# A transformer stack's feed-forward second projections as seven block products of 2x2 blocks

## The chip, the cores and the metric

One core of a Trainium2 chip runs the whole program. The time is device microseconds (us) of one execution, the median of several runs. Engines: TensorE (PE in the profile, PEld its weight loads), VectorE (DVE), ScalarE (ACT), GpSimd (POOL), SyncE (SP, which issues the weight loads from DRAM).

## The reference

512 tokens of width 1024 pass through two blocks of one kind and one of a second kind, all in float32. Each has a token mixer (attention) and feed-forwards; what the change touches are the four feed-forwards. Cut to these, with `rms_norm` and the convolution as in the model:

```python
def conv_ffn(h, w_up, conv_w, conv_b, w_down):      # twice: f0, f1
    u = h @ w_up                                    # 512x1024 @ 1024x5632
    u = causal_conv_of_width_3(u, conv_w) + conv_b  # per channel, along tokens
    gate, up = jnp.split(u, 2, axis=-1)
    return (jax.nn.gelu(gate, approximate=True) * up) @ w_down   # 512x2816 @ 2816x1024

def _swiglu(x, w_gate, w_up, w_down):               # twice: s0, s1
    return (jax.nn.silu(x @ w_gate) * (x @ w_up)) @ w_down

x = x + rms_norm(f, g_post)      # f: a feed-forward's result; 0.5 * in s0 and s1
h = rms_norm(x, g_pre_of_next)
```

## The kernel before, in words

Stages run in the order m0, f0, m1, f1, s0, m2, s1: m are the mixers, f the feed-forwards with convolution and gelu, s those with silu. Every float32 operand of a matmul is held as a high part (rounded to the matmul's format fp32r) and a low part (the rest), and each product of two tiles is three matmuls: high x high, high x low, low x high (`mm3`, L223 to L225). The high part of a tile is a copy on ScalarE, the low part a difference on VectorE (`split2`, L231 and L232; for weights `_split`, L112, and `flush`, L121).

**Weights** come through one stream. `Weights` holds a list of chunks (1 MB in DRAM, loaded by SP into two raw buffers `wraw`) and of units (128x1024, in one of four slots `whi`, `wlo`). A unit's place in the list is the order of its use. When the last unit of a chunk has its low part, SP is told to load the chunk after the next into that buffer (`_load`, from `flush`). `ahead` splits units while slots are free.

**A feed-forward** (`ffn`) goes through its 22 inner tiles of 128 in two parts of 11 (`reg_ffn`). For each inner tile, a gate tile and an up tile (128 inner x 512 tokens) are summed over 8 k-tiles in a PSUM bank. `convd` (L622 to L624) makes the convolution with one ScalarE and two VectorE passes; then come gelu on ScalarE, and `gg = cg * cu` on GpSimd (L641). Without convolution, silu on ScalarE and `gg = cg * PS` on VectorE (L643). `split2` puts the tile into `gh` and `gl`. At the part's end `out_part` makes the second projection: for each half of the 1024 output columns, four token tiles x 11 inner tiles x 3 matmuls of 128x128 by 128x512. The first part's result is copied to `part`; the second part's is added to it (`post1`: addition L672, ScalarE's sum of squares L673, the product with the gain L674, on VectorE for the first half and on GpSimd for the second).

**The junction.** In the second half of the last part (`out_last`) the weights' low parts go to GpSimd (`W.defer`, `W.lo`), three more slots are lent for the next stage's first weights, and as each token tile is complete, `finish` (L574 to L587) makes the root of its mean square (L580, L326, L582), adds the scaled result to x in two halves (L585), and `pre_norm` makes the normed row `hn` for the next stage (L335 square sum, L339). `turn` (L380) transposes hn on TensorE, and `evacuate` splits the transposed tile into `Hh` and `Hl`. The next stage starts with tokens 0 and 1 (L422, L460) while 2 and 3 are finished.

Every engine takes its instructions in the order in which the program issues them; no scheduler reorders them.

Of the kernel before, what the change touches and what calls it, by code (L numbers as in the profile page):

```python
# [16 lines left out]
T = 512  # L17
# [10 lines left out]


class Weights:  # L30

# [5 lines left out]
    def __init__(self, nc, pool):  # L37
        self.nc = nc
        self.raw = [pool.tile([128, 2048], F32, name=f"wraw{i}") for i in range(self.NRAW)]
        self.free = self.slots(pool, self.NHL, "w")  # L40
        self.extra, self.first, self.limit = [], 0, 0
        self.where = {}
        self.chunks = []
        self.units = []
        self.loaded = 0
# [25 lines left out]
    def add(self, srcs, a, b, unit_slices):  # L71
        c = len(self.chunks)
        self.chunks.append((srcs, a, b))
        for n, (a0, a1, b0, b1) in enumerate(unit_slices):
            self.units.append((c, a0, a1, b0, b1, n == len(unit_slices) - 1))

# [26 lines left out]
    def _split(self):  # L103
        u = self.split
        c, a0, a1, b0, b1, last = self.units[u]
        _, a, b = self.chunks[c]
        if c >= self.loaded:
            self.flush()
        raw = self.raw[c % self.NRAW][:, :a * b].rearrange("p (a b) -> p a b", a=a)[:, a0:a1, b0:b1]
# [3 lines left out]
        self.late.append((lo, raw, hi, c + self.NRAW if last else 0))  # L113
        self.split += 1
        if not self.defer:
            self.flush()

    def flush(self):

        for lo, raw, hi, nxt in self.late:  # L120
            self.lo.tensor_sub(lo, raw, hi.bitcast(F32))  # L121
            self._load(nxt)
        self.late = []

    def ahead(self, keep=1):

        self.flush()
        while self.split < len(self.units):
# [8 lines left out]
    def view(self, u):  # L137
        _, a0, a1, b0, b1, _ = self.units[u]
        n = (a1 - a0) * (b1 - b0)
        return tuple(t[:, :n].rearrange("p (a b) -> p a b", a=a1 - a0) for t in self.where[u])  # L140

# [32 lines left out]
class Net:  # L174
# [418 lines left out]
    def reg_ffn(self, wg, wg0, wu, wu0, wd):  # L593
        W = self.W
        for k0, nk in ((0, 11), (11, 11)):
            for j in range(k0, k0 + nk, 2):
                m = min(2, k0 + nk - j)
                W.cols(wg, wg0 + j * 128, m * 128)
                W.cols(wu, wu0 + j * 128, m * 128)
            for h in range(2):  # L600
                W.rows(wd, k0, nk, h * 512, 512)

    def ffn(self, conv, half, last, gpost, gpre_next):
# [3 lines left out]
        with ExitStack() as st:  # L607
            P = st.enter_context(self.tc.tile_pool(name="ffn", bufs=1))
            gh = P.tile([128, 11, T], F32R, name="gh")
            gl = P.tile([128, 11, T], F32R, name="gl")  # L610
            part = P.tile([128, 4, D], F32, name="part")
            tmp = ExitStack()
            Q = tmp.enter_context(self.tc.tile_pool(name="ffntmp", bufs=1))
            cg = [Q.tile([128, T], F32, name=f"cg{i}") for i in range(3)]
            gg = [Q.tile([128, T], F32, name=f"gg{i}") for i in range(2)]
            if conv is not None:
                cu = [Q.tile([128, T], F32, name=f"cu{i}") for i in range(3)]
                cw = Q.tile([128, 2 * NFT, 4], F32, name="cw")
                nc.gpsimd.dma_start(cw, conv)

            def convd(dst, ps, j):
# [4 lines left out]
            def post_g(j):  # L626
                def f(ps):
                    c = cg[j % 3]
                    if conv is not None:
                        convd(c, ps, j)  # L630
# [5 lines left out]
            def post_u(j, jj):  # L636
                def f(ps):
                    g = gg[j % 2]
                    if conv is not None:
# [9 lines left out]
            sst = self.sm(8)  # L649
            for p in range(2):  # L650
                k0 = p * 11
                for jj in range(0, 11, 2):
                    m = min(2, 11 - jj)
                    posts = [post_g(k0 + jj + e) for e in range(m)] + [post_u(k0 + jj + e, jj + e) for e in range(m)]
                    if p == 0 and jj == 0:
# [3 lines left out]
                    for f in posts:  # L659
                        self.gemm_T(f, soon=True)  # L660
                if p == 0:
                    for h in range(2):
                        def post0(i, ps):
                            if i % 2:
                                nc.vector.tensor_copy(part[:, i, h * 512:h * 512 + 512], ps)
                            else:
                                nc.scalar.activation(part[:, i, h * 512:h * 512 + 512], ps, AF.Copy)
                        self.out_part((gh, gl), 11, post0)
                else:
                    def post1(i, ps, h):  # L670
                        f = part[:, i, h * 512:h * 512 + 512]
                        nc.vector.tensor_add(f, ps, f)  # L672
                        nc.scalar.activation(ps, f, AF.Square, accum_out=sst[:, h * 4 + i:h * 4 + i + 1])  # L673
                        (nc.gpsimd if h else nc.vector).tensor_mul(f, f, self.gpost[:, h * 512:h * 512 + 512])  # L674

                    tmp.close()
                    with self.tc.tile_pool(name="more", bufs=1) as M:
                        self.W.lend(self.W.slots(M, 3, "m"), 9)
                        self.out_last((gh, gl), 11, lambda i, ps: post1(i, ps, 0), lambda i, ps: post1(i, ps, 1),
                                      lambda i: self.finish(i, part[:, i, :512], part[:, i, 512:], sst[:, i:i + 1],  # L680
                                                            sst[:, 4 + i:5 + i], half, last))
                        self.W.give_back()
                    while self.side:
                        self.pump()

# [1068 lines left out]
```

## Time and profile before

| | |
|---|---|
| median of 3 runs | 2851.55 us (2850.07 to 2852.74) |
| the profiled execution | 2851.37 us |
| its span, first to last instruction | 2849.4 us |
| TensorE busy | 2790.2 us (98%), 14196 matmuls |
| VectorE, ScalarE, GpSimd busy | 1397.4, 1102.0, 365.3 us |
| mean granted TensorE clock | 0.995 |
| DMA | 255.45 MB, mean 90 GB/s |

The page gives each engine's busy time; the timeline lists instructions with their start, their duration and, in brackets, how long the engine was idle before and which operand came last; the waits group such idle times. TensorE's matmuls overlap, so one's duration (0.39) is longer than the distance of two starts.

### The profile page before, as it was taken

To read this page: it belongs to the slowest core of one execution; us is meant where nothing else is said; L and a number is where in the kernel's file an instruction comes from. 1 tells how busy PE (TensorE), PEld (TensorE's weight loads), DVE (VectorE), ACT (ScalarE), POOL (GpSimd) and SP (SyncE) were. 2 spreads that over 40 slices of the span, in tenths; PEclk is the share of its full clock that TensorE was granted. 3 is DMA by queue.
4 is the path that set the end of the run, shared out by engine and by line. 5 is a ranking of instruction groups with operands and counts; after the bars stand their busy time and mean duration, and the time that the engine had idled before them with its cause. 6 is when DMAs were issued, how large, how long until landed. Compare 5 with 4: busy or idle time off the path is not lost.

```text
span 2849.4 us, 34641 instructions
## 1 busy us (share of the span) xinstructions
PE 2790.2 (98%) x14196; PEld 2282.4 (80%) x14196; DVE 1397.4 (49%) x2126; ACT 1102.0 (39%) x1886; POOL 365.3 (13%) x285
## 2 busy tenths in 40 slices
PE   8999999999999999999999999999999999999998
PEld 7778688888878787788888888888777978888887
DVE  4666645535555666455535453233653343533334
ACT  3444634423444456444334332223343322432232
POOL 5221100100122221000101110000522000000000
PEclk9999999999999999999999999999999999999999
DMA  4211132333322111233332323323421223322332
GB/s 148 74 57 34 34 130 86 105 115 108 111 71 91 60 38 45 82 119 95 108 103 91 110 89 100 100 81 118 140 74 53 72 78 97 111 94 92 104 97 73
DMA packets 234318, 255.45 MB, mean 90 GB/s; under 512 B 33072, under 2 KB 193184, under 8 KB 233776
## 3 DMA queue, kind: packets, MB, share of 16 engines
q1 hardware_dynamic: 228016, 233.53, 25.7%
q0 software_dynamic: 4992, 16.94, 1.9%
q8 instruction: 111, 1.82, 0.3%
q10 hardware_dynamic: 1152, 2.77, 0.3%
q14 instruction: 47, 0.39, 0.0%
HBM read 248.60 MB, written 5.53 MB: 89 GB/s over the span
## 4 chain that ended last, share of the span: by engine, by line
PE 90%; DVE 5%; ACT 3%; issue 1%; DMA 0%; DVEq 0%; ACTq 0%; POOL 0%; POOLq 0%
PE PS L223 26%; PE PS L225 25%; PE PS L224 25%; PE PS L422 2%; DVE x L585 2%; PE PS L1124 1%; PE PS L1110 1%; PE PS L1080 1%; PE PS L425 1%; PE PS L460 1%; DVE hn L339 1%; PE PS L1220 1%; PE PS L1192 1%; PE PS L380 1%; PE PS L1511 1%
## 5 line engine op out<-in xcount | busy, mean ns | idle before, releaser
L121 DVE TENSOR_TENSOR wlo<-wraw,whi 128x1024 fp32r<-128x1024 f32 (+3 forms) x366 | 440.3, 1208 | 726.5 <-ACT whi L112 726.4
L223 PE MATMUL PS<-Hh,whi 128*128 128x512 f32 x1952 | 776.1, 398 | 4.1 <-DVE oBl L232 2.8
L225 PE MATMUL PS<-Hh,wlo 128*128 128x512 f32 x1952 | 761.0, 390 | 0.9 <-DVE wlo L121 0.9
L224 PE MATMUL PS<-Hl,whi 128*128 128x512 f32 x1952 | 760.6, 390 | 0.0
L112 ACT ACTIVATE whi<-wraw 128x1024 fp32r<-128x1024 f32 (+2 forms) x432 | 436.9, 1016 | 340.0 <-PE PS L225 279.5
L223 PEld LDWEIGHTS PS<-Hh,whi 128*128 128x128 f32 x1952 | 366.5, 188 | 88.3 <-issue 8.7
L225 PEld LDWEIGHTS PS<-Hh,wlo 128*128 128x128 f32 x1952 | 366.4, 188 | 79.2 <-DVE wlo L121 1.5
L224 PEld LDWEIGHTS PS<-Hl,whi 128*128 128x128 f32 x1952 | 367.0, 188 | 70.5
L121 POOL TENSOR_TENSOR wlo<-wraw,whi 128x1024 fp32r<-128x1024 f32 (+1 forms) x66 | 162.8, 2467 | 1268.1 <-ACT whi L112 1268.1
L223 PE MATMUL PS<-whi,gh 128*128 128x512 f32 x624 | 242.8, 389 | 0.0
L224 PE MATMUL PS<-wlo,gh 128*128 128x512 f32 x624 | 242.7, 389 | 0.0
L225 PE MATMUL PS<-whi,gl 128*128 128x512 f32 x624 | 242.7, 389 | 0.0
L231 ACT ACTIVATE gh<-gg 128x512 fp32r<-128x512 f32 x88 | 55.7, 632 | 327.2 <-DVE gg L643 178.9
L223 PEld LDWEIGHTS PS<-whi,gh 128*128 128x128 f32 x624 | 117.3, 188 | 24.3
L225 PEld LDWEIGHTS PS<-whi,gl 128*128 128x128 f32 x624 | 117.1, 188 | 24.4
L224 PEld LDWEIGHTS PS<-wlo,gh 128*128 128x128 f32 x624 | 117.1, 188 | 24.4
L641 POOL TENSOR_TENSOR gg<-cg,cu 128x512 f32<-128x512 f32 x44 | 56.7, 1289 | 549.4 <-DVE cu L624 549.4
L232 DVE TENSOR_TENSOR gl<-gg,gh 128x512 fp32r<-128x512 f32 x88 | 60.9, 693 | 125.6 <-ACT gh L231 125.6
L223 PE MATMUL PS<-whi,Hh 128*128 128x512 f32 (+2 forms) x320 | 118.2, 369 | 1.9 <-ACT whi L112 1.6
L224 PE MATMUL PS<-wlo,Hh 128*128 128x512 f32 (+2 forms) x320 | 116.7, 365 | 0.5 <-DVE wlo L121 0.5
L225 PE MATMUL PS<-whi,Hl 128*128 128x512 f32 (+2 forms) x320 | 116.5, 364 | 0.0
L1091 DVE TENSOR_REDUCE small<-PS 128x2 f32<-128x256 f32 (+3 forms) x64 | 52.7, 824 | 72.0 <-PE PS L1082 61.2
(355 smaller groups left out, 3966.0 us busy)
## 6 DMA issues: line engine op xcount, KB each, us to landing
wraw<-in_w_in_dram SPq DMA_DIRECT2D x56, 1024.0 KB, 5.0
wraw<-in_w_up_dram SPq DMA_DIRECT2D x40, 1024.0 KB, 5.1
wraw<-in_ffn_w_gate_dram SPq DMA_DIRECT2D x20, 1024.0 KB, 5.2
wraw<-in_ffn_w_up_dram SPq DMA_DIRECT2D x20, 1024.0 KB, 5.3
wraw<-in_w_down_dram SPq DMA_DIRECT2D x16, 1024.0 KB, 5.0
wraw<-in_ffn_w_down_dram SPq DMA_DIRECT2D x16, 1024.0 KB, 5.0
wraw<-in_w_out_dram SPq DMA_DIRECT2D x12, 1024.0 KB, 4.9
wraw<-in_w_down_dram SPq DMA_DIRECT2D x8, 768.0 KB, 4.3
```

Source lines behind the costliest of these rows:

```text
L112: self.nc.scalar.activation(hi, raw, AF.Copy)
L121: self.lo.tensor_sub(lo, raw, hi.bitcast(F32))
L223: mm(out, lh, rh, start=start, stop=False)
L224: mm(out, lh, rl, start=False, stop=False)
L225: mm(out, ll, rh, start=False, stop=stop)
L231: nc.scalar.activation(hi, src, AF.Copy)
L232: nc.vector.tensor_sub(lo, src, hi.bitcast(F32))
L339: nc.vector.scalar_tensor_tensor(hn, self.x[:, i], r, self.gpre, op0=OP.mult, op1=OP.mult)
L422: self.nc.tensor.matmul(ps[:, sl], ww[:, k], self.Hh[:, k, sl], start=k == 0 and ww is w[0], stop=False)
L585: nc.vector.scalar_tensor_tensor(x, f, r, x, op0=OP.mult, op1=OP.add)
L641: nc.gpsimd.tensor_mul(g, cg[j % 3], cu[j % 3])
L1091: nc.vector.reduce_max(m, S2, axis=AX.X, negate=True)
```

## The change

The second projection of one part, G (512 tokens x 2P inner tiles) times W (2P inner tiles x 1024), is taken as 2x2 blocks: tokens 0 to 255 and 256 to 511; even and odd inner tiles; columns 0 to 511 and 512 to 1023. With A11, A12 (tokens' first half, even and odd tiles), A21, A22, and B11 to B22, seven products of blocks make the four blocks of the result (Winograd's form):

S1 = A21 + A22, S2 = S1 - A11, S3 = A11 - A21, S4 = A12 - S2; T1 = B12 - B11, T2 = B22 - T1, T3 = B22 - B12, T4 = B21 - T2. In the order of the program: product 0 A11 x B11 (bank pair a), 1 S1 x T1 (b), 2 S2 x T2 (onto a), 3 S4 x B22 (onto b), 4 A12 x B21 (c), 5 S3 x T3 (onto a), 6 A22 x T4 (onto a).

A product is two token tiles x P pairs of inner tiles x 3 matmuls. For this the parts become three, of 6, 8 and 8 inner tiles (P = 3, 4, 4).

- The sums S are four GpSimd operations of 128x256 for each pair of inner tiles (L773 to L778), in the buffers `hn`, and are split with A11, A12 and A22 into `Ah` and `Al`. Splits are issued one tile later (`late`, `run_late`).
- The differences T are GpSimd operations in the raw buffers (L114, L115, L116, L118). B11 and B12 come by the stream; B22 and B21 are loaded into `tm`, the buffers of cg, cu and gg, when the part's last tile is through (`open_quad`, L130). The weight units of a part are, in order, B11, T1, T2, B22, B21, T3, T4, two to each at P = 4.
- After each product its bank is copied to or added to `part` (L701, L703, L705); the result blocks that need no further product are finished (`fin`) after products 3, 4, 5 and 6.
- In the last part low parts go to GpSimd from product 4 on; three of `Ah`/`Al`'s operands that are done are lent as slots; tokens 0 and 1 are transposed in product 6.

```diff
-        for k0, nk in ((0, 11), (11, 11)):
+        for k0, nk in self.PARTS:
...
-            for h in range(2):
-                W.rows(wd, k0, nk, h * 512, 512)
+            W.quad(wd, k0, nk // 2)
...
+        order(b11, [lambda i: sub(b11(i), b12(i), b11(i))])
+        order(b11, [lambda i: when_open(lambda: sub(b11(i), b22(i), b11(i)))()])
+        order(b11, [lambda i: sub(b12(i), b22(i), b12(i))])
+        order(b22, [])
+        order(b21, [lambda i: sub(b21(i), b21(i), b11(i)), lambda i: self._load(c + 2) if i == last else None])
+        order(b12, [lambda i: self._load(c + 3) if i == last else None])
+        order(b21, [])
...
+        steps = ((0, a, False, 0, 0, True, False), (3, b, False, 1, 1, True, False), (4, a, True, 0, 1, True, False),
+                 (6, b, True, 0, 1, False, True), (1, c, False, 0, 0, False, True), (5, a, True, 1, 1, False, True),
+                 (2, a, True, 1, 0, True, True))
+        for n, (op, banks, on, row, h, new, end) in enumerate(steps):
+            ws = [W.get() for _ in range(nu)]
+            if fin and n == 4:
+                W.defer, W.lo = True, nc.gpsimd
+            W.ahead(0, u0 + nu * (n + 2) if fin and n < 4 else 1 << 30)
+            for e in range(2):
+                i, ps = 2 * row + e, banks[e]
...
+                f = part[:, i, h * 512:h * 512 + 512]
+                if new and first:
...
+                else:
+                    nc.vector.tensor_add(f, ps, f)
+                if fin:
+                    if n == 6:
+                        self.turn(0)
+                    if end:
+                        fin(i, h, c[e] if n == 5 else ps)
+                    self.pump()
+                    self.evacuate()
+                    W.flush()
...
-                    self.split2(gh[:, jj], gl[:, jj], g)
+                    if jj % 2 == 0:
+                        nc.gpsimd.tensor_sub(s[:, 2], g11, g21)
+                        late.append(lambda: self.split2(Ah[:, 0, m], Al[:, 0, m], g11))
+                    else:
+                        nc.gpsimd.tensor_add(s[:, 0], g21, g22)
+                        nc.gpsimd.tensor_sub(s[:, 1], s[:, 0], g11)
+                        nc.gpsimd.tensor_sub(s[:, 3], g12, s[:, 1])
+                        late.append(lambda: self.split2(Ah[:, 1:3, m], Al[:, 1:3, m], g.rearrange("p (h t) -> p h t", h=2)))
+                        late.append(lambda: self.split2(Ah[:, 3:7, m], Al[:, 3:7, m], s))
```

How instructions stand on three engines, in the order in which they are issued (line, operation, output and inputs, size):

GpSimd, in f0 of the kernel before: the gate-up products up to the end of the last part, with nothing between them, then the junction's low parts and gain products.

```order
L641 TENSOR_TENSOR gg_3440<-cg_3439,cu_3444 128x512
L641 TENSOR_TENSOR gg_3441<-cg_3437,cu_3442 128x512
L121 TENSOR_TENSOR wlo_69<-wraw_64,whi_68 128x1024
L674 TENSOR_TENSOR part<-part,gpost 128x512
L121 TENSOR_TENSOR wlo_73<-wraw_64,whi_72 128x1024
```

GpSimd, at the end of f0's first part after the change: T1 (L114), the last two tiles' products (L767) and sums (to `hn`), then T2 (L115), T3 and T4.

```order
L114 TENSOR_TENSOR wraw_64<-wraw_65,wraw_64 128x1024
L114 TENSOR_TENSOR wraw_64<-wraw_65,wraw_64 128x512
L767 TENSOR_TENSOR tm<-tm 128x512
L773 TENSOR_TENSOR hn_77<-tm 128x256
L767 TENSOR_TENSOR tm<-tm 128x512
L776 TENSOR_TENSOR hn_77<-tm 128x256
L777 TENSOR_TENSOR hn_77<-hn_77,tm 128x256
L778 TENSOR_TENSOR hn_77<-tm,hn_77 128x256
L115 TENSOR_TENSOR wraw_64<-tm,wraw_64 128x1024
L115 TENSOR_TENSOR wraw_64<-tm,wraw_64 128x512
L116 TENSOR_TENSOR wraw_65<-tm,wraw_65 128x1024
L116 TENSOR_TENSOR wraw_65<-tm,wraw_65 128x512
```

The sums of the last pair now stand between its product and the first matmul that needs S, and T2 stands right behind them.

ScalarE, in the last part of f0 before, from the next stage's first weights on.

```order
L112 ACTIVATE whi_68<-wraw_64 128x1024
L112 ACTIVATE whi_72<-wraw_64 128x1024
L673 ACTIVATE PS,small<-part 128x512
L326 ACTIVATE small<-small 128x1
L335 ACTIVATE hn_77,small<-x 128x1024
L326 ACTIVATE small<-small,eps 128x1
L112 ACTIVATE whi_70<-wraw_65 128x1024
```

ScalarE there after the change: squares of the second half (L802), T3 from `wraw_65`, T4 from `tm`, the next stage's first unit from `wraw_64`, and only then the square of token 0's first half.

```order
L802 ACTIVATE PS,small<-part 128x512 x2
L169 ACTIVATE Ah<-wraw_65 128x1024 x2
L169 ACTIVATE Ah<-tm 128x1024
L169 ACTIVATE whi_72<-tm 128x1024
L169 ACTIVATE whi_70<-wraw_64 128x1024
L802 ACTIVATE PS,small<-part 128x512
L383 ACTIVATE small<-small 128x1
L802 ACTIVATE PS,small<-part 128x512
L392 ACTIVATE hn_77,small<-x 128x1024
```

The next stage's first high part stood ahead of the first token's square before too, but now its load is issued behind T4's last difference.

VectorE, in the last part of f0 before: one token's finish, and the additions of the next tokens' tiles.

```order
L672 TENSOR_TENSOR part<-PS,part 128x512
L580 TENSOR_SCALAR small<-small 128x1
L582 RECIPROCAL small<-small 128x1
L585 SCALAR_TENSOR_TENSOR x<-part,small,x 128x512 x2
L672 TENSOR_TENSOR part<-PS,part 128x512
L338 RECIPROCAL small<-small 128x1
L339 SCALAR_TENSOR_TENSOR hn_77<-x,small,gpre 128x1024
```

VectorE there after the change: additions of products 3 and 4 (x3), finish of token 0, second addition of product 4, finish of token 1, and then the addition of product 5's first bank, which product 6 uses again.

```order
L705 TENSOR_TENSOR part<-PS,part 128x512 x3
L803 TENSOR_TENSOR part<-part,gpost 128x512
L637 TENSOR_SCALAR small<-small 128x1
L639 RECIPROCAL small<-small 128x1
L642 SCALAR_TENSOR_TENSOR x<-part,small,x 128x512 x2
L705 TENSOR_TENSOR part<-PS,part 128x512
L803 TENSOR_TENSOR part<-part,gpost 128x512
L637 TENSOR_SCALAR small<-small 128x1
L639 RECIPROCAL small<-small 128x1
L642 SCALAR_TENSOR_TENSOR x<-part,small,x 128x512 x2
L705 TENSOR_TENSOR part<-PS,part 128x512
L395 RECIPROCAL small<-small 128x1
```

Two tokens' finishes stand ahead of an addition for which a bank is wanted; before, the banks of a half were not used again by its own products.

Over the whole program TensorE has 264 matmuls fewer; VectorE goes from 1905 to 2053 rows of this kind, ScalarE from 1392 to 1512, GpSimd from 251 to 504.

## Rows read from the trace of the kernel before

**Rows 1.** The page's first part: busy us, share of the span, instructions.
```profile
PE 2790.2 (98%) x14196; PEld 2282.4 (80%) x14196; DVE 1397.4 (49%) x2126; ACT 1102.0 (39%) x1886; POOL 365.3 (13%) x285
```
**Rows 2.** Timeline: start, us, engine, line, operation, [idle before <-releaser]; f0's second projection starts.
```profile
588.50 0.39 PE L223 MATMUL PS<-whi,gh 128*128 128x512 f32 x1
...
595.98 0.39 PE L223 MATMUL PS<-whi,gh 128*128 128x512 f32 x1
...
588.82 0.76 ACT L622 ACTIVATE cu<-PS,cw 128x512 f32<-128x512 f32 x1
```
**Rows 3.** Waits of PE: us in total, times, longest; 813 to 850, then 1630 to 1655.
```profile
PE PS L380 <- DVE small L580: 2.2, 2, 1.9
PE PS L460 <- POOL wlo L121: 1.5, 1, 1.5
PE PS L460 <- ACT Hh L231: 0.8, 1, 0.8
...
PE PS L380 <- DVE small L580: 3.8, 2, 1.9
PE PS L422 <- ACT Hh L231: 1.1, 1, 1.1
```
**Rows 4.** Timeline of ACT, DVE and POOL, one up tile of f0.
```profile
730.14 0.78 ACT L622 ACTIVATE cu<-PS,cw 128x512 f32<-128x512 f32 x1 [1.42 <-PE PS L225]
...
730.96 0.75 DVE L623 SCALAR_TENSOR_TENSOR cu<-PS,cw,cu 128x511 f32<-128x511 f32 x1 [0.97 <-ACT cu L622]
731.74 0.75 DVE L624 SCALAR_TENSOR_TENSOR cu<-PS,cw,cu 128x510 f32<-128x510 f32 x1
...
732.66 1.30 POOL L641 TENSOR_TENSOR gg<-cg,cu 128x512 f32<-128x512 f32 x1 [14.69 <-DVE cu L624]
```
**Rows 5.** Timeline of DVE, one up tile of s0.
```profile
1761.65 0.69 DVE L643 TENSOR_TENSOR gg<-cg,PS 128x512 f32<-128x512 f32 x1 [1.88 <-PE PS L225]
```
**Rows 6.** Groups by form: line, engine, operation, xcount | busy us, mean ns | idle before.
```profile
L112 ACT ACTIVATE whi<-wraw 128x1024 fp32r<-128x1024 f32 x392 | 410.2, 1050 | 281.7 <-PE PS L225 235.4 <-issue 18.9 <-DMA wraw<-in_w_up_dram 9.4
...
L121 POOL TENSOR_TENSOR wlo<-wraw,whi 128x1024 fp32r<-128x1024 f32 x65 | 161.0, 2477 | 1256.2 <-ACT whi L112 1256.2
L641 POOL TENSOR_TENSOR gg<-cg,cu 128x512 f32<-128x512 f32 x44 | 56.7, 1289 | 549.4 <-DVE cu L624 549.4
...
L871 POOL TENSOR_TENSOR kr<-gpost,t 128x128 f32<-128x128 f32 x24 | 11.0, 460 | 40.9 <-DVE t L867 40.9
...
L121 DVE TENSOR_TENSOR wlo<-wraw,whi 128x1024 fp32r<-128x1024 f32 x327 | 411.2, 1262 | 658.0 <-ACT whi L112 657.9
```
**Rows 7.** Timeline: DVE and POOL at f0's junction; last row the program's end, POOL idle.
```profile
813.78 0.69 DVE L672 TENSOR_TENSOR part<-PS,part 128x512 f32<-128x512 f32 x1 [4.84 <-PE PS L225]
...
815.79 4.16 DVE L585 SCALAR_TENSOR_TENSOR x<-part,small,x 128x512 f32<-128x512 f32 x2
...
816.56 2.85 POOL L121 TENSOR_TENSOR wlo<-wraw,whi 128x1024 fp32r<-128x1024 f32 x1
...
2829.88 2.02 DVE L585 SCALAR_TENSOR_TENSOR x<-part,small,x 128x512 f32<-128x512 f32 x2
```
**Rows 8.** The page's DMA issues: output<-input, queue, xcount, KB, median us to landing.
```profile
wraw<-in_w_down_dram SPq DMA_DIRECT2D x16, 1024.0 KB, 5.0
```
**Rows 9.** Timeline of PE behind a wait; then a window: us, busy (x), PEclk, DMA.
```profile
823.12 1.44 PE L380 MATMUL PS<-cf,hn 128*128 128x128 f32 x8 [1.90 <-DVE small L580]
...
824.78 0.63 PE L224 MATMUL PS<-mlo,gh 128*128 128x512 f32 x1
...
827.23 0.39 PE L224 MATMUL PS<-mlo,gh 128*128 128x512 f32 x1
...
823.70:827.00 3.30, 3.30 (x12) 2.71 (x11) 3.30 (x2) 0.00 (x0) 3.30 (x2) 0.50 0.01 4
```
**Rows 10.** Timeline of POOL and PE: the fourth weight unit at m1's start.
```profile
837.37 2.81 POOL L121 TENSOR_TENSOR wlo<-wraw,whi 128x1024 fp32r<-128x1024 f32 x1
...
840.24 0.50 PE L460 MATMUL PS<-wlo,Hh 128*128 128x512 f32 x1 [1.47 <-POOL wlo L121]
```

More of the change, by code (lines that the diff above doesn't have):

```diff
@@ L27, with __init__ @@
 PI = 3.141592653589793
+class Quad:
+    def __init__(self):
+        self.room, self.late = None, []
 class Weights:
@@ L44, in __init__ @@
         self.units = []
+        self.quads = []
         self.loaded = 0
@@ new lines, in quad, with when_open, order @@
+    def quad(self, w, k0, P):
+        v = w.rearrange("(k p) n -> p k n", p=128)
+        block = lambda o, h: v[:, k0 + o:k0 + 2 * P:2, h * 512:h * 512 + 512]
+        c, q = len(self.chunks), Quad()
+        self.chunks += [([(0, 128, block(0, h))], P, 512) for h in range(2)]
+        q.blocks = [block(1, 1), block(1, 0)]
+        q.P = P
+        sub = self.nc.gpsimd.tensor_sub
+        part = [slice(i, min(i + 2, P)) for i in range(0, P, 2)]
+        b11 = lambda i: self.raw_of(c)[:, part[i]]
+        b12 = lambda i: self.raw_of(c + 1)[:, part[i]]
+        b22 = lambda i: q.room[i][:, :part[i].stop - part[i].start]
+        b21 = lambda i: q.room[2 + i][:, :part[i].stop - part[i].start]
+        def when_open(f):
+            return lambda: f() if q.room else q.late.append(f)
+        def order(src, after, chunk=c + 1):
+            for i, s in enumerate(part):
+                self.units.append((chunk, lambda i=i: src(i), s.stop - s.start, 512, [lambda i=i, f=f: f(i) for f in after]))
+        last = len(part) - 1
+        order(b11, [lambda i: sub(b11(i), b12(i), b11(i))])
[5 more added lines that the diff above has]
+        order(b21, [])
+        self.quads.append(q)
@@ L77, in cols, with open_quad @@
+    def open_quad(self, room):
+        q = self.quads.pop(0)
+        q.room = room
+        for b, block in enumerate(q.blocks):
+            for i in range(0, q.P, 2):
+                m = min(2, q.P - i)
+                self.nc.sync.dma_start(room[2 * b + i // 2][:, :m], block[:, i:i + m])
+        for f in q.late:
+            f()
+        return q.P
     def cols(self, w, c0, n):
@@ L112, in _split @@
         self.nc.scalar.activation(hi, raw, AF.Copy)
-        self.late.append((lo, raw, hi, c + self.NRAW if last else 0))
+        self.late.append((lo, raw, hi, after))
         self.split += 1
@@ L118, in flush, with ahead @@
     def flush(self):
-        for lo, raw, hi, nxt in self.late:
+        late, self.late = self.late, []
+        for lo, raw, hi, after in late:
             self.lo.tensor_sub(lo, raw, hi.bitcast(F32))
-            self._load(nxt)
-        self.late = []
-    def ahead(self, keep=1):
+            for f in after:
+                f()
+    def ahead(self, keep=1, upto=1 << 30):
         self.flush()
-        while self.split < len(self.units):
+        while self.split < min(upto, len(self.units)):
             extra = self.extra and self.first <= self.split < self.limit
@@ L137, in view @@
     def view(self, u):
[L138 to L140 removed]
+        _, _, a, b, _ = self.units[u]
+        return tuple(t[:, :a * b].rearrange("p (a b) -> p a b", a=a) for t in self.where[u])
     def get(self):
@@ L660, in ffn, with fin @@
                         self.gemm_T(f, soon=True)
[L661 to L684, printed above, removed]
+                run_late()
+                e = (k0 + nk - 2) % 3
+                room = [tm[:, 2 * i:2 * i + 2] for i in ((e + 2) % 3, e, (e + 1) % 3, 3)]
+                def fin(i, h, sq):
+                    f = part[:, i, h * 512:h * 512 + 512]
+                    nc.scalar.activation(sq, f, AF.Square, accum_out=sst[:, h * 4 + i:h * 4 + i + 1])
+                    (nc.gpsimd if h else nc.vector).tensor_mul(f, f, self.gpost[:, h * 512:h * 512 + 512])
+                    if h == 0:
+                        self.side.append(self.finish(i, part[:, i, :512], part[:, i, 512:], sst[:, i:i + 1],
+                                                     sst[:, 4 + i:5 + i], half, last))
+                self.down(Ah, Al, room, part, p == 0, fin if k0 + nk == NFT else None)
+            while self.side:
+                self.pump()
     def proj(self, nk, mov, post):
```

84 lines of the change are left out of this document (63 added, 21 removed).

## Prediction

> **What bounds the kernel now.** I read the page's shares first: the matmul engine is busy for 98% of the span, VectorE for 49%, ScalarE for 39%, GpSimd for 13% [rows 1]. The kernel is as long as its matmuls plus the few waits among them. So three questions follow: how long one matmul takes, where TensorE waits now, and who would make it wait after. The first is answered by starts, not by durations, since matmuls overlap: 33 of 128x512 lie between two starts 7.48 us apart, 0.2267 us each [rows 2]. The second is answered by the waits at the end of an FFN [rows 3]: 4.5 us at the first junction, 4.9 at the second, and the third shows the first two rows of the first again, 3.7: 13.1 us in all. Through an FFN's middle TensorE waits for nothing.
>
> **What is removed.** A second projection has 22 inner tiles x 4 token tiles x 2 halves x 3 = 528 matmuls; seven block products instead of eight leave 462. Four FFNs: 264 x 0.2267 = **-59.9 us**, all on the path, as nothing else bounds the middle of an FFN. The old junctions go too: their 13.1 us, and 2 x 1.2 of low clock behind the two longest waits (see the clock below): **-15.5**.
>
> **What is added** are sums on GpSimd and short products. The four weight differences (T1 to T4), 11 pairs of inner tiles each, and four sums per pair of tiles of the activations, run while TensorE works; GpSimd, 13% busy, has room in the mean. But a product is short: 24 matmuls, 5.44 us, at 4 pairs, and 18, 4.08 us, at 3. A wait is the time at which its operand comes less the time at which TensorE wants it.
>
> *Start of product 1 (S1 x T1), 12 times.* Take the start of product 0 as zero; the last up tile has just left TensorE. With the convolution, ScalarE, two VectorE passes and GpSimd's product follow one another: 730.14 to 733.96 [rows 4], so with 0.32 until the first starts (588.50 to 588.82 [rows 2]) the product ends at 4.1. Behind it GpSimd makes three sums of 128x256. No row has that size: 128x128 takes 0.46 and 128x512 1.29 [rows 6]; I take 0.74 an estimate midway, so S is there at 6.4. ScalarE's high part of 1024 elements takes 1.05, VectorE's low part 1.26 [rows 6], and behind that on VectorE stands the low part of T1's second half (1.26 at 4 pairs, at 3 as long as the 128x512 of VectorE, 0.69 [rows 7]). With nothing in the way these end at 7.5, 8.7 and 9.9 (9.3). TensorE wants T1's second half at 5.44 + 1.36 + 0.23 = 7.0 (at 3 pairs 5.7): waits of 2.9 and 3.6. But T2's difference is issued on GpSimd right behind the sums, and takes 2.4 to 2.8. Two VectorE operations with both inputs in SBUF took 4.16 beside GpSimd and 2.02 without it [rows 7], and GpSimd's own difference there 2.85. By this, VectorE's low part starts when GpSimd's difference ends, at 8.9 instead of 7.5: waits of 4.4 and 5.1. I take these, 2 x (5.1 + 4.4 + 4.4) = **+27.8**; lower end 18.8. Without the convolution VectorE makes the product from PSUM in 0.69 [rows 5], so sums end at 3.2; by the same steps the waits are 1.1 at 4 pairs and 1.9 at 3: 2 x (1.9 + 1.1 + 1.1) = **+8.2**, lower end 1.
>
> The Trainium skill, "SBUF — State Buffer", sections "SBUF: two separate sides" and "Who interferes with whom", says that a VectorE operation with two SBUF inputs and a GpSimd operation that reads SBUF share one port pair, held by one of them for a whole instruction while the other stands still. The trace agrees where it can (4.16 against 2.02 [rows 7]); taken at every overlap of this change the rule gives the upper ends of products 2, 5 and 6 below, 9.6 + 3.6 + 16 = 29 us more than I sum, an estimate of 2925; it speaks against a change that moves sums to GpSimd.
>
> *Product 2, 12 times:* T2's second half, through the same queue, is 0 to 1.5 late; 0.7 each, **+8.4**.
>
> *Product 5, last part, 4 times.* From product 4 on low parts go to GpSimd, 2.48 each [rows 6]. From the start of product 4 it has T4's second difference (2.4), two gain products (1.29 each) and two low parts of T3: 9.9 us, when TensorE wants the first low part at 5.7. Ends 1.8 (first alone, 7.5) and 4.2 (both); I take 3.3, **+13.2**.
>
> *Product 6, last part, 4 times.* It adds to the banks of product 5, so it waits until VectorE has read them, and that addition stands on VectorE behind the finish of tokens 0 and 1; their first step needs ScalarE's squares, which stand behind the high part of the next stage's first weights, whose load is issued only after T4's last difference. Counted from the start of product 3: high and low parts of B21 and two additions, 5.0; two differences and the gain products between them, to 11.4 (13 when they stand still beside VectorE); load 5.0 [rows 8]; high part 1.05; square and small steps from there 1.4; the two x operations 2.0 (4.2 beside GpSimd [rows 7]), small steps of token 1, 2.0, counted as between 813.78 and 815.79 [rows 7], its x operations 2.0 (4.2) and the addition 0.7: 25.6 to 31.6. Product 5 ends at 3 x 5.44 = 16.3, with its own wait at 19.6. So 6 to 12 us; I take 8, nearer to the lower end, as VectorE's two pairs are seldom both held, for the three with a next stage. The last FFN has no load nor high part: 6.0 less, 0 to 6; 2. **+26.** This is the largest wait, and what is late there is no arithmetic but a queue's order.
>
> *Start of the next stage, 3 times.* Now 0.8 to 1.1 for the transposed activations [rows 3]. Four copies and four differences of 128x512 for two tokens now lie there together, 2.1 and 2.8: ends 1 and 5, I take 2.5, **+7.5**. *Fourth weight unit, at two of them* (the stages that begin with token tiles): its high part stands on ScalarE behind the squares of tokens 2 and 3, then comes a low part on GpSimd, 2.8 [rows 10]. Two finishes and the rest end 11.6 to 15.4 after the stage's start, and TensorE comes there after three units of 12 matmuls, 8.2: 3.5 to 7; I take 6, **+12**. Today's such unit is 1.47 late [rows 10].
>
> *Clock.* After its 1.9 us wait and eight transposes TensorE ran at granted clock 0.50, the 1.2 GHz level, for 3.3 us [rows 9]: six matmuls between 824.78 and 827.23 took 2.45 instead of 1.36, and with the one ahead of them some 1.2 us are lost. Some 12 of the new waits are as long: **+14.4**; 0 to 34. *Tail* of the last tokens: +2.
>
> Sum: -59.9 - 15.5 + 27.8 + 8.2 + 8.4 + 13.2 + 26 + 7.5 + 12 + 14.4 + 2 = +44.1. The profiled execution took 2851.4, the median of the runs is 2851.6, 0.2 apart, so the sum needs no shift: **2896 us**. With all lower ends (no standing still of VectorE, no clock loss) 2833; with all upper ends 2954. Adding, multiplying and loading more costs nothing elsewhere: VectorE's and ScalarE's 120 to 150 more rows lie beside TensorE's 98%, and the loads of B21 and B22, 5.0 us each [rows 8], are issued when the part's last up tile is through, needed two products later.
>
> **Rivals.** *Queues only.* VectorE and GpSimd seldom meet; the order of queues remains. Then all terms but the clock are at their lower ends: 2833 + 14.4 = 2847, with 2833 to 2870 about it. For it: VectorE is idle for half of the time. Against: S's chain puts GpSimd's T2 exactly beside VectorE's low part, in 12 of 12 parts. 0.17, of it 0.08 faster, 0.04 within, 0.05 slower. *Faster.* The same, and product 6 isn't late either: that decides at one place, whether the addition of product 5's first bank is through VectorE by the time product 5 ends. If T4's differences run two products earlier than I count, the load lands while product 3 runs, squares aren't late, and 18 us more go: 2833 - 18 = 2815. For it: all difference operands are in SBUF by product 2. Against: B21's parts are made only when product 2's slots are free. 0.15. *Clock.* Each of about 37 short waits costs 1.2 instead of 12: 30 more, and with longer waits above 2955: for it, 1.9 us sufficed once [rows 9]; against, most waits are under 2. 0.08. *The change does not do what it says:* the order of the rows has 264 matmuls fewer on TensorE, so this has no chance of its own.
>
> **Numbers.** Forecast 2896, its own band 2870 to 2955, 0.60; queues only 0.17; faster 0.15; clock 0.08. A measurement of this kernel can tell some 0.2%, 5.7 us, from no change. Faster by more: 0.15 + 0.08 = 0.23; within: 0.04, and 0.01 of the forecast's edge: 0.05; slower: 0.72. The range 2830 to 2955 leaves out most of the faster case and the clock case, 0.2.
>
> **What would show it.** Right: TensorE busy some 60 us less in the middle of FFNs, with waits for VectorE's low parts (wlo and Al) at the second product of each part, 4 to 5 us with convolution and 1 to 2 without; one wait of about 8 us for a `part` addition at the seventh product of f0, f1 and s0; x operations at 4 beside GpSimd. Wrong: if these second products start within 1 us, VectorE isn't held; if the seventh products start without a wait, the load was early; if the matmuls' own starts lie further apart than 0.2267 for long stretches, it is the clock.

## The result

The changed kernel takes 2941.76 us (median of 4, 2940.91 to 2942.62) against 2851.91 us before: ratio 1.0316, 95% interval 1.0298 to 1.0334, 90 us slower. Slower was forecast, by 44 us; the time lies within the range that was given (to 2955), the loss is twice the forecast.

The page's first part, for [rows 1]:

```profile
PE 2778.3 (95%) x13932; PEld 2255.0 (77%) x13932; DVE 1650.5 (56%) x2330; ACT 1203.1 (41%) x2002; POOL 836.0 (28%) x573
```

264 matmuls are gone, and TensorE is busy for 12 us less only, since matmuls at a low clock last longer. The mean granted clock is 0.977, it was 0.995. By the two pages VectorE has 204 instructions more, ScalarE 116 and GpSimd 288, where 148, 120 and 253 rows were counted ahead. The waits of TensorE over the whole span (us in total, times, longest):

```profile
PE PS L690 <- DVE wlo L179: 22.5, 18, 2.0
PE PS L690 <- DVE small L395: 21.6, 3, 7.5
PE PS L690 <- ACT whi L169: 18.7, 8, 4.7
PE PS L690 <- ACT Ah L288: 18.4, 6, 5.9
PE PS L690 <- POOL Al L179: 9.9, 7, 2.1
```

L690 is the matmul of the block products. The first row lies in products 1 and 2 of a part, the third in product 1, the fourth in product 0, the second is product 6, the fifth product 5. Where [rows 3] had three junctions with 4 to 5 us, every part now has waits, and the fourth row, six waits of up to 5.9 us for A11, is one that the prediction did not have. It is seen in f0's first part (timeline: start, us, engine, line, operation, idle before and its releaser):

```profile
541.23 0.80 PE L690 MATMUL PS<-whi,Ah 128*128 128x512 f32 x1 [5.93 <-ACT Ah L288]
...
551.69 0.50 PE L690 MATMUL PS<-wlo,Ah 128*128 128x512 f32 x1 [1.90 <-DVE wlo L179]
...
519.09 0.42 ACT L288 ACTIVATE Ah<-tm 128x256 fp32r<-128x256 f32 x1 [3.40 <-POOL tm L767]
...
540.76 0.42 ACT L288 ACTIVATE Ah<-tm 128x256 fp32r<-128x256 f32 x1 [2.90 <-POOL tm L767]
541.09 0.77 ACT L746 ACTIVATE tm<-PS,cw 128x512 f32<-128x512 f32 x1
...
538.62 2.11 POOL L767 TENSOR_TENSOR tm<-tm 128x512 f32<-128x512 f32 x1 [0.30 <-DVE tm L748]
...
547.59 2.37 POOL L115 TENSOR_TENSOR wraw<-tm,wraw 128x1024 f32<-128x1024 f32 x1
...
548.75 2.29 DVE L289 TENSOR_TENSOR Al<-hn,Ah 128x1024 fp32r<-128x1024 f32 x1 [2.53 <-ACT Ah L288]
```

TensorE began product 0 at 533.78, its last up tile being done. That tile's convolution (L746) starts at 541.09, 7.3 us later, where the prediction put 0.32. ScalarE waited for GpSimd's product of the tile before, to split A11 (L288), and the convolution stood behind that split. That wait is 2.90 us; the rest of the 7.3 had built up at tiles before, where splits stand in the same way (3.40 at 519.09). The last two rows show what is called the port below, VectorE standing still beside GpSimd, as forecast: T2's difference and S's low part side by side, 2.29 instead of 1.26.

GpSimd stands still too, which the prediction's chain for product 1 left out: it counted GpSimd's product (L767) at 1.30, and here that product takes 2.11 beside a low part of VectorE, 2.03 in the mean (1.29 in [rows 6], 1.30 again in e13):

```profile
L767 POOL TENSOR_TENSOR tm<-tm 128x512 f32<-128x512 f32 x44 | 89.2, 2027 | 343.1 <-DVE tm L748 343.1
```

Product 6's wait, with what stands ahead of the addition (L705) that frees its bank:

```profile
838.03 1.06 ACT L169 ACTIVATE whi<-wraw 128x1024 fp32r<-128x1024 f32 x1 [2.63 <-DMA wraw<-in_w_in_dram]
839.00 0.58 ACT L802 ACTIVATE PS<-part 128x512 f32<-128x512 f32 x1
...
841.45 4.89 DVE L642 SCALAR_TENSOR_TENSOR x<-part,small,x 128x512 f32<-128x512 f32 x2
...
849.72 1.41 DVE L642 SCALAR_TENSOR_TENSOR x<-part,small,x 128x512 f32<-128x512 f32 x2
...
851.05 0.68 DVE L705 TENSOR_TENSOR part<-PS,part 128x512 f32<-128x512 f32 x1
...
851.88 0.77 PE L690 MATMUL PS<-Ah 128*128 128x512 f32 x1 [7.45 <-DVE small L395]
```

It is the chain that was forecast: the next stage's first weights wait for their load, the square stands behind them, the x operations of token 0 take 4.89 beside GpSimd (those of token 1, with GpSimd idle, 1.41), and the addition comes after two finishes.

From the starts of the matmuls, less 0.2267 us for each, the loss is: products 0 and 1 with convolution 66.7 us, product 1 without 12.3, product 2 8.6, products 5 and 6 48.4 (transposes taken off), the stage starts 28.4, the end 1.8. That is 166.2; less 59.9 of matmuls and 16.7 that the junctions of before cost: +89.6. Low clock behind a wait is in these terms; a wait by itself is, below, the distance of two starts less 0.2267.

### The profile page after: what moved, and what is told of

Read it like the earlier page. It is cut to its first block, busy times and chain, and to the rows that moved or that the text cites. A ratio compares the mean times of both kernels' runs of the same rounds, so it can differ in the third digit from the quotient of the medians.

```text
span 2939.1 us, 35002 instructions
## 1 busy us (share of the span) xinstructions
PE 2778.3 (95%) x13932; PEld 2255.0 (77%) x13932; DVE 1650.5 (56%) x2330; ACT 1203.1 (41%) x2002; POOL 836.0 (28%) x573
## 5 line engine op out<-in xcount | busy, mean ns | idle before, releaser
L169 ACT ACTIVATE whi<-wraw 128x1024 fp32r<-128x1024 f32 (+3 forms) x436 | 438.8, 1014 | 338.4 <-PE PS L281 80.4
L690 PE MATMUL PS<-whi,Ah 128*128 128x512 f32 x568 | 231.9, 408 | 37.1 <-ACT whi L169 18.7
L690 PE MATMUL PS<-wlo,Ah 128*128 128x512 f32 x568 | 231.5, 408 | 22.5 <-DVE wlo L179 22.5
L690 PE MATMUL PS<-whi,Al 128*128 128x512 f32 x568 | 228.5, 402 | 0.0
L767 POOL TENSOR_TENSOR tm<-tm 128x512 f32<-128x512 f32 x44 | 89.2, 2027 | 343.1 <-DVE tm L748 343.1
L690 PEld LDWEIGHTS PS<-whi,Ah 128*128 128x128 f32 x568 | 111.4, 196 | 67.1 <-ACT whi L169 22.4
L690 PEld LDWEIGHTS PS<-wlo,Ah 128*128 128x128 f32 x568 | 111.9, 197 | 53.1 <-DVE wlo L179 29.8
L690 PEld LDWEIGHTS PS<-whi,Al 128*128 128x128 f32 x568 | 111.5, 196 | 24.7 <-DVE Al L289 1.4
L289 DVE TENSOR_TENSOR Al<-hn,Ah 128x1024 fp32r<-128x1024 f32 x44 | 66.7, 1517 | 98.5 <-ACT Ah L288 98.5
L705 DVE TENSOR_TENSOR part<-PS,part 128x512 f32<-128x512 f32 x136 | 90.5, 682 | 53.1 <-PE PS L690 53.1
L288 ACT ACTIVATE Ah<-tm 128x256 fp32r<-128x256 f32 x88 | 45.5, 517 | 170.7 <-POOL tm L767 140.9
```

The lines of the kernel that those rows point to most:

```text
L288: nc.scalar.activation(hi, src, AF.Copy)
L289: nc.vector.tensor_sub(lo, src, hi.bitcast(F32))
L690: nc.tensor.matmul(ps, lhs[l], w[r][:, m % 2], start=not on and m + x == 0, stop=m == P - 1 and x == 2, skip_group_check=on)
```

## Experiments

Two theories at first. **Queues and chains:** a wait is the length of a chain of instructions through the in-order queues of ScalarE, GpSimd and VectorE, less the work TensorE has in the meantime. **Port:** VectorE stands still beside GpSimd. A third is the **clock**, which I had counted as a cost of its own.

**e1: the last tile's convolution first.**

```diff
                     g = gg[j % 2]
+                    if conv is not None:
+                        convd(cu[j % 3], ps, NFT + j)
                     run_late()
                     if conv is not None:
-                        convd(cu[j % 3], ps, NFT + j)
                         nc.gpsimd.tensor_mul(g, cg[j % 3], cu[j % 3])
...
```
(and the same in `post_g`.) 

> In the two feed-forwards with convolution the splits of the tile before are issued behind a tile's convolution instead of ahead of it; same instructions, another order on ScalarE and VectorE. Queue theory (the last up tile's convolution starts 7 us late because ScalarE's split of A11, which waits for GpSimd, stands ahead of it): the waits of products 0 and 1 there, 19.4 + 30.1 us of the changed kernel's trace, fall to about half and the low clock behind them with it: 2900 to 2920 us. Port theory (GpSimd's sums and differences hold VectorE up, whatever the order): within 8 us of 2942.

2918.03 us, ratio 1.0224 (1.0195 to 1.0254): 24 us less, by one order, in the queue theory's range. The convolution now starts 0.20 us after product 0:

```profile
532.57 0.39 PE L690 MATMUL PS<-whi,Ah 128*128 128x512 f32 x1
...
532.77 0.78 ACT L746 ACTIVATE tm<-PS,cw 128x512 f32<-128x512 f32 x1 [3.71 <-PE PS L282]
533.45 0.41 ACT L288 ACTIVATE Ah<-tm 128x256 fp32r<-128x256 f32 x1
...
540.51 2.28 DVE L289 TENSOR_TENSOR Al<-hn,Ah 128x1024 fp32r<-128x1024 f32 x1 [2.54 <-ACT Ah L288]
542.72 0.68 DVE L179 TENSOR_TENSOR wlo<-wraw,whi 128x512 fp32r<-128x512 f32 x1
```

Product 0's waits fell from 19.4 to 3.8 us, product 1's only from 30.1 to 23.5: S is still late, and its low part still takes 2.28. The queue theory holds for product 0.

**e2: squares ahead of the next stage's weights.**

```diff
-            W.ahead(0, u0 + nu * (n + 2) if fin and n < 4 else 1 << 30)
+            W.ahead(0, u0 + nu * min(n + 2, 7) if fin and n < 5 else 1 << 30)
```


> In the last part the next stage's first weights are split one product later, so that ScalarE's squares of tokens 0 and 1 no longer stand behind them. Queue theory (product 6 waits 7.6, 7.6 and 6.9 us in f0, f1 and s0 because of the load these weights wait for): these waits fall to 2 to 4 us, 2920 to 2930 us. Port theory (the finish is slow because its x operations take 4.9 us beside GpSimd): the waits stay over 6, 2937 to 2943 us.

2941.73 us, 1.0307 (1.0278 to 1.0337): nothing won. The time is in the port theory's range, but its condition, that the waits stay over 6 us, is not met; the queue theory had the waits and missed the time. TensorE's waits at f0's junction, of the changed kernel, then of e2:

```profile
PE PS L690 <- DVE small L395: 7.5, 1, 7.5
PE PS L690 <- POOL Al L179: 2.8, 2, 2.1
PE PS L517 <- DVE Hl L289: 2.7, 1, 2.7
```
```profile
PE PS L517 <- DVE Hl L289: 6.5, 1, 6.5
PE PS L690 <- POOL Al L179: 3.2, 3, 1.8
```

Product 6's wait for VectorE is gone there, as the queue theory had it, and came back where the next stage begins (L517): the next stage needs the same tokens' finish.

**e3: matmuls of no use in the waits.** Between 6 and 28 each time, ahead of the waiting matmuls of products 0, 1 and 6 (the counts are cut here):

```diff
+                    for _ in range(self.filler(fin, n, e, m, P)):
+                        nc.tensor.matmul(c[0] if n < 2 else b[0], Ah[:, 0, 0, 0:128], ws[0][0][:, 0], start=True, stop=True)
```


> Matmuls of no use (24, or 4 to 28) are put ahead of the matmuls that wait in products 0, 1 and 6, as long as those waits or a little shorter; the result is the same. Clock theory (behind these waits TensorE runs at 1.2 GHz and pays again): the low stretches behind products 0, 1 and 6 go, some 9 stretches with about 21 us lost, 2920 to 2930 us. Queue theory with a clock that costs nothing of its own (what is lost in product 0 is taken off the wait in product 1): 2936 to 2944 us.

2944.13 us, 1.0316 (1.0286 to 1.0346). The mean clock rose from 0.977 to 0.988, so some 65 us less were run at 1.2 GHz, and none of it was won. Windows of f0's first part (us, busy of PE, PEld, DVE, ACT, POOL, then PEclk), the changed kernel, then e3, and e3's end of product 1's wait:

```profile
540.00:547.00 7.00, 5.77 (x14) 4.55 (x15) 2.79 (x4) 1.72 (x3) 4.66 (x6) 0.51 0.26 71
```
```profile
540.00:547.00 7.00, 6.49 (x28) 4.78 (x28) 2.79 (x4) 1.72 (x3) 4.66 (x6) 1.00 0.27 75
...
551.68 0.50 PE L703 MATMUL PS<-wlo,Ah 128*128 128x512 f32 x1 [1.92 <-DVE wlo L179]
```

At full clock TensorE gets through product 0 earlier and waits longer for T1: the matmul behind that wait starts at 551.68, with the slow clock at 551.69. VectorE's and ScalarE's chain sets the time. At f0's junction product 6 is through earlier too, and the next stage waits longer, where the changed kernel has 2.7:

```profile
PE PS L517 <- DVE Hl L289: 5.1, 1, 5.1
```

So in products 0, 1 and 6 the lost clock is no term to add to waits that follow one another; e3 leaves product 5 and the stage starts as they are.

**e4: no differences.** `sub` does nothing, so T1 to T4 are left out. 

> The four weight differences T1 to T4 are left out (their buffers hold plain blocks of the weights); products, loads and splits stay. Port theory: product 2's waits (7.3 us), product 5's (11.3) and 1 us of each product 1 go, and the next stage's load is issued 5.6 us earlier, so most of product 6's; with the clock 50 to 60 us: 2882 to 2892 us. Queue theory: the waits of products 0 and 1 with convolution (49.5 us and their clock) stay over 35 us, and the time falls by 25 to 45: 2897 to 2917 us.

2909.80 us, 1.0196 (1.0166 to 1.0225): 32 us, in the queue theory's range. Product 2's waits went, products 0 and 1 with convolution kept 41.6 of 49.5. Product 6 in f0 waited 7.6 still, though ScalarE waited for no load there any more. The addition came 13.8 us after product 5's start instead of 16.3, and product 5 itself was through 2.5 us earlier: T4 and the load, to which I had put the wait down, only add to a chain that is long without them.

**e5: two token tiles in turn**, on top of e1.

```diff
-            for e in range(2):
+            pairs = [(e, m) for m in range(P) for e in range(2)] if n < 3 else [(e, m) for e in range(2) for m in range(P)]
+            for e, m in pairs:
...
```


> On top of e1: in products 0 to 2 the two token tiles alternate over the pairs of inner tiles instead of one after the other, so the last pair's operands are wanted 1.4 to 2.0 us later and a product's second half of weights 1.4 later; same instructions otherwise. Chain theory (a wait is the chain through ScalarE, GpSimd and VectorE from the last up tile, less the work that TensorE has until then; low clock is not a cost of its own): product 0's 3.8 us go, product 1's 23.5 with convolution fall to about 11, its 9.7 without to about 1, product 2's 6.4 to 0: 2888 to 2897 us. Port theory (VectorE stands still beside GpSimd and gets further behind): 2910 to 2918 us.

2906.75 us, 1.0195 (1.0165 to 1.0224): 11 of the 21 to 30 us that the chain theory wanted, between the two. Product 0's waits went; in products 1 and 2 T1's and T2's second halves are now wanted late enough only in part: VectorE's low parts still show 33 waits, 21.6 us in all.

**e6: low parts of the last part on VectorE**, on top of e1.

```diff
-                W.defer, W.lo = True, nc.gpsimd
+                W.defer, W.lo = True, nc.vector
```


> On top of e1: in the last part the low parts from product 4 on stay on VectorE instead of GpSimd. Port theory (the x operations take 4.9 instead of 2.0 us because GpSimd makes low parts beside them): product 5's waits (11.5 us) go, the x operations take about 2 each pair, products 6 and stage starts win 4 to 6 us per junction: 2885 to 2900 us. Queue theory (VectorE's low parts now stand ahead of the finish, and what is won at products 5 and 6 comes back at the next stage's start): 2908 to 2920 us.

2899.75 us, 1.0170 (1.0141 to 1.0200): 18 us, just inside the port theory's range. But the idle time ahead of product 6 at the three junctions grew (26.7 us, 21.7 in e1); the gain is in product 5, which waits no more, and at the stage starts.

**e7: seven products in two parts only**, on top of e5; the last part and the junction as in the kernel before.

```diff
-                self.down(Ah, Al, room, part, p == 0, fin if k0 + nk == NFT else None)
+                if k0 + nk < NFT:
+                    self.down(Ah, Al, room, part, p == 0)
+                    continue
...
+                self.out_last((gh, gl), 8, lambda i, ps: post1(i, ps, 0), lambda i, ps: post1(i, ps, 1),
...
```


> On top of e5: only the first two parts (14 inner tiles) go by seven products, the last part of 8 inner tiles and the junction are as in the kernel before, so 168 matmuls are saved instead of 264, 38.1 us. Chain theory, with two causes that add: the junctions cost as before (nothing new) and the first two parts keep 10 to 15 us of waits: 2825 to 2842 us. If the first two parts' waits don't shrink by the order of e5 they keep 27 and the time is 2843 to 2855 us.

2847.01 us, 0.9980 (0.9969 to 0.9991), 60 us below e5 although it has 96 matmuls more (21.8 us). So the last part by seven products loses 82 us in waits and in what they delay. In the first two parts 20.8 us of idle time remained, 25 as waits are counted above, where e1 had 29: the order of e5 shortened them little, and the time is in the range given for that case.

**e8: sums on VectorE**, on top of e1: `nc.gpsimd` becomes `nc.vector` in the four sums. 

> On top of e1: the four activation sums of a pair go to VectorE instead of GpSimd. Chain theory: three sums in the chain take about 0.4 instead of 0.7 to 1.1 us each, so S is 1 to 1.5 us earlier in each of 12 parts: 2900 to 2910 us. Port theory: VectorE, with two SBUF inputs, stands beside GpSimd's products and differences instead, and its queue gets longer: 2914 to 2930 us.

2903.94 us, 1.0185 (1.0155 to 1.0214), in the chain theory's range, but not by all 12 parts. All of the gain lies in s0 and s1, whose first two parts took 29.5 and 38.5 us (matmuls alone 28.6 and 38.1); with convolution the first two did not get shorter.

**e9: T1's second half first**, on top of e5: `W.ahead(0)` ahead of a part's last `run_late()`. 

> On top of e5: one call ahead of the last splits of a part, so that ScalarE and VectorE split T1's second half before they wait for S instead of after. Chain theory: product 1 then waits for S alone; its waits fall by 1 to 2 us in each of 12 parts: 2888 to 2899 us. If T1's second half is late for its own reason (its slot, its difference on GpSimd), nothing changes: 2903 to 2909 us.

2898.13 us, 1.0161 (1.0140 to 1.0181): 8.6 us, as the chain theory had it.

**e10: e7, e8 and e9 together.** 

> e7 (seven products in the first two parts only) with the sums on VectorE as in e8 and T1's second half first as in e9. Chain theory: of the 20.8 us that TensorE waited inside the seven products of e7 at most 5 are left, and the junctions stay: 2824 to 2834 us, faster than the kernel before. Port theory: VectorE, which now makes the sums beside GpSimd's differences, keeps the waits: 2840 to 2850 us.

2850.61 us, 0.9992 (0.9983 to 1.0002): no gain over e7, 0.6 above the port theory's range. f0's first part, VectorE and GpSimd:

```profile
538.47 2.60 DVE L814 TENSOR_TENSOR hn<-tm 128x256 f32<-128x256 f32 x1 [1.18 <-POOL tm L799]
541.10 0.42 DVE L815 TENSOR_TENSOR hn<-hn,tm 128x256 f32<-128x256 f32 x1
541.56 0.42 DVE L816 TENSOR_TENSOR hn<-tm,hn 128x256 f32<-128x256 f32 x1
...
538.40 2.39 POOL L115 TENSOR_TENSOR wraw<-tm,wraw 128x1024 f32<-128x1024 f32 x1
```

Three sums of one size: the first began 0.07 behind T2's difference and ended 0.3 behind it, 2.60 us; the others took 0.42. That is the port by itself, and it falls into the chain of S.

**e11: all three parts by seven products with all these orders.** 

> All three parts by seven products, with every order found so far: e5, e8, e9, low parts of the last part on VectorE as in e6, and the next stage's weights one product later as in e2. If the last part's loss lies in products 5 and 6 alone, 2840 to 2858 us. If it lies in the finish of four tokens that all come late (the seven products give no token's row before product 4), the waits move to the next stage's start and the time stays at 2862 to 2885 us, above e10.

2884.96 us, 1.0115 (1.0094 to 1.0135): at the upper end of the second case.

After these, what was open was the port's share. **e12: the changed kernel with T2 to T4 on VectorE.**

```diff
-        order(b11, [lambda i: when_open(lambda: sub(b11(i), b22(i), b11(i)))()])
-        order(b11, [lambda i: sub(b12(i), b22(i), b12(i))])
+        order(b11, [lambda i: when_open(lambda: vsub(b11(i), b22(i), b11(i)))()])
+        order(b11, [lambda i: vsub(b12(i), b22(i), b12(i))])
```
(and T4's, the same.) 

> The changed kernel with the differences T2, T3 and T4 on VectorE instead of GpSimd, nothing else. Port theory: no low part stands still beside them; product 2's waits (7.3 us) go, product 1's fall by 1 us each, product 5's by half, and 10 us of clock and junction with them: 2912 to 2928 us, near e4, where they are left out (2910). Queue theory: VectorE's queue is longer by 1.2 us for each difference, what is won is lost again: 2935 to 2950 us.

2931.85 us, 1.0278 (1.0258 to 1.0299): 10 us, between the two. S's low part by form, the changed kernel, then e12:

```profile
L289 DVE TENSOR_TENSOR Al<-hn,Ah 128x1024 fp32r<-128x1024 f32 x44 | 66.7, 1517 | 98.5 <-ACT Ah L288 98.5
```
```profile
L289 DVE TENSOR_TENSOR Al<-hn,Ah 128x1024 fp32r<-128x1024 f32 x44 | 53.9, 1225 | 98.5 <-ACT Ah L288 98.5
...
L115 DVE TENSOR_TENSOR wraw<-tm,wraw 128x1024 f32<-128x1024 f32 x20 | 24.4, 1221 | 0.3
```

The mean fell to 1225 ns, so nothing stands still there any more; but products 0 and 1 with convolution kept 49.7 us of waits: there ScalarE's late start comes before T2's difference.

**e13: e10 with T2 to T4 on VectorE.** 

> e10 with T2 to T4 on VectorE. Port theory: the four parts with convolution take 31 to 33 and 40 to 41 us instead of 38.4 to 39.6 and 45.4 to 45.8, those without keep 29.4 and 38.5: 2822 to 2834 us, the fastest of all. Queue theory: the parts with convolution keep over 36 and 44 us, since VectorE has the sums, splits and differences one after the other: 2843 to 2853 us.

**2829.90 us, 0.9921 (0.9904 to 0.9937): 23 us faster than the kernel before, 112 than the changed one**, in the port theory's range. The same place as in e10:

```profile
540.33 0.42 DVE L814 TENSOR_TENSOR hn<-tm 128x256 f32<-128x256 f32 x1 [1.18 <-POOL tm L799]
540.79 0.43 DVE L815 TENSOR_TENSOR hn<-hn,tm 128x256 f32<-128x256 f32 x1
...
542.80 1.22 DVE L289 TENSOR_TENSOR Al<-hn,Ah 128x1024 fp32r<-128x1024 f32 x1
```

s0's and s1's parts take 28.6 and 38.1 us, their matmuls alone. With convolution they take 34.0 to 35.2 and 40.3 to 40.4: the 4-pair parts as expected, the 3-pair parts 1 to 2 us above it.

**e14: e11 with T2 to T4 on VectorE.** 

> e11 with T2 to T4 on VectorE. The first two parts should win as in e13, some 20 us. If the last part loses by the port too, it comes down to 47 us and less and the time to 2835 to 2850 us. If it loses by the finish of four tokens that all come late, it keeps over 50 us in f0, f1 and s0 and the time is 2852 to 2870 us, above e13.

2858.35 us, 1.0011 (1.0001 to 1.0021), 27 below e11 and 28 above e13, in the second case. The last part takes 53.0, 54.0 and 50.9 us in f0, f1 and s0 (its matmuls 38.1, the transposes of two tokens 2.1); the longest waits are all there and at the starts of stages:

```profile
PE PS L690 <- DVE Al L179: 16.4, 5, 4.4
PE PS L690 <- DVE small L395: 9.4, 3, 3.8
PE PS L517 <- ACT whi L169: 6.6, 2, 5.4
```

So the last part still loses with T2 to T4 and its low parts off GpSimd. The longest row is T3's low parts, which stand on VectorE among the finishes here; these orders with the low parts on GpSimd were not run. In seven products no token's row is complete before product 4, so four finishes come in a burst that nothing is left to cover; that this burst, and not a single order in it, is the cause is what e2, e6, e11 and e14 have in common, but no run takes the burst alone away, so it is argued, not shown.

## Why the prediction was wrong

*What was removed* is right: the matmuls' distance stayed 0.2267 us, and without waits the parts of e13 take what the counts say.

*Start of product 1 with convolution* is the step that failed: +27.8 was forecast, and products 0 and 1 cost 66.7, clock included, 49.5 of it waits. That is 39 of the 45 us by which the sum is short. "So with 0.32 until the first starts" took the distance from [rows 2], where nothing stands ahead of the convolution on ScalarE. The change puts splits there that wait for GpSimd; ScalarE's queue runs behind, and at a part's end that lag is paid: 7.3 us instead of 0.32, and product 0, for which no wait was counted, waits for A11 as well. That splits are issued one tile later, and so ahead of the last convolution, was known; the order was looked at on GpSimd there, and not on ScalarE. e1 takes this order away and nothing else: 24 us fewer. What was worked out behind the 0.32 then holds: T1's second low part is done 10.8 us after product 0's start (543.40 less 532.57), as 5.7 and a wait of 5.1 had it, and products 0 and 1 have 27.3 us of waits. That this is so near to 27.8 is in part luck: 3.8 of it are in product 0, and half of product 1's idle time is for ScalarE's high part of T1's second half, which the chain left out. The port's part of the same step, S's low part held until T2's difference is done, is right: 2.29 against 1.22 in e13.

*Without convolution* 8.2 was forecast, 12.3 measured, 1.6 of it low clock. *Product 2*: 8.4 forecast, 8.6 measured, but by luck: it was spread over 12 parts, and 6.9 of it lie in the six without convolution. *Product 5*: 13.2 forecast, 11.3 of waits. *Product 6*: 26 forecast, 24.7 of waits (7.6, 7.6, 6.9, 2.5). The size is right and the cause half: e4 has the wait without the load. And it is no lone term, since e2 moved it to the next stage. Its x operations were counted at 2.0 without GpSimd, from the last row of [rows 7]; but GpSimd was not idle there, its gain product runs beside the first of the two until 2830.69, and a pair with GpSimd idle takes 1.41.

```profile
2829.40 1.29 POOL L674 TENSOR_TENSOR part<-part,gpost 128x512 f32<-128x512 f32 x1 [347.40 <-ACT PS L673]
```

*Stage starts and the fourth unit*: 19.5 forecast, 28.4 measured, clock included.

*Clock*: 14.4 forecast as a term of its own; at half the clock that is 29 us of low stretches, and they grew from some 29 to 136 us (twice the span times what the mean clock lacks to 1). e3 shows that where waits follow one another this is not added to them. The terms in this text hold it, wherever no later wait took it back.

Of the rivals, *queues only* and *faster* fall: VectorE does stand beside GpSimd (e10, e12), and product 6 does wait. *Clock* had it right that more low clock comes than was counted (107 us more, against 29), but not that this costs 30 us more: 65 us fewer at 1.2 GHz won nothing in e3. Of the signs named, the x operations at 4.9 beside GpSimd and 7 us at the seventh product were seen. The second product waited as long as named, but with convolution mostly for ScalarE's high part of T1's second half (18.2 of 26.8 us of idle time), not for VectorE's low part. TensorE's busy time fell by 12 us, not 60. The Trainium skill, "SBUF — State Buffer", section "Who interferes with whom", agrees with e10 and e13 (2.60 beside GpSimd, 0.42 without); by its rule alone I had estimated 2925, 17 below the measured time. No run splits those 17 us; the order of e1 alone is worth more than them.

## What to carry to other kernels

Before a chain is timed from the end of a matmul group, look at what stands ahead of its first instruction on that engine's queue: a split that waits for a slow engine delays everything issued behind it, and at the end of a loop the lag is paid in full. A saving of matmuls by sums of blocks pays where the operands come early and nothing needs the rows one by one; here that was in two parts of three (e13), with the sums and T2 to T4 on VectorE, so that neither engine holds up the other in the chain of S. Mend the orders and the port together before judging either: in the changed kernel moving the differences won 10 us, with the orders mended 21 (e10 to e13) and 27 (e11 to e14).

## What was not expected of the hardware

71 instead of 136 us at the 1.2 GHz level won nothing (e3): where the two traces were laid side by side, TensorE was not the last to come behind those stretches. And a 128x256 operation of VectorE took 2.60 us beside one of GpSimd and 0.42 after it (e10), so a small operation can pay nearly the whole of a large one. GpSimd pays as well: its 128x512 product took 2.03 us in the mean instead of 1.29.
